# A weight gradient by two-level block products: a new order of visits, and three results stored in halves of columns

## The chip, the core and the metric

The kernel runs on one core of a Trainium2 chip. The metric is device microseconds of that core. Before the change the median of three runs is 162.01 us (161.97 to 162.06).

## The reference

```python
"input": np.random.randn(16, 512, 1024).astype(np.float32)
"grad_output": np.random.randn(16, 512, 768).astype(np.float32)
...
grad_weight = np.einsum('bmk,bmn->kn', input, grad_output)
return grad_weight.astype(np.float32)
```

The batch and the rows fold into one: a product of X transposed (8192 rows by 1024 columns) with G (8192 rows by 768 columns), summed over the 8192 rows. The result is 1024 by 768 in float32, 3.15 MB; the inputs are 58.72 MB.

## The kernel before

**Loads.** The rows come as 32 loads of 256 rows, numbered 0 to 31 (the string `LOADS`). Loads 0 to 3 and 31 are of kind "s": their two groups of 128 rows are multiplied plainly. Loads 4 to 30 are of kind "P": one level of a fast block scheme (seven products in place of eight) is taken over them. GpSimd's queue (POOL) issues the loads with a cast to bfloat16 (lines 170, 171, and 175, 177 for the first ones); each waits for the one eight places before it to land, and later for a free buffer. Only the first 256 rows of X and the first 128 of G come in float32, over the ScalarE and SyncE queues (`xf`, `gf`), and are rounded on the core (line 217).

**Blocks.** The result has four quarters: A, B (first half of the rows), C, D (second half); A and C are the left 384 columns, B and D the right. Each quarter has four blocks of 128 rows, so that C2 is the third block of C. On a "P" load seven products run: A, B, C, and four that feed several quarters, called 1, 5, 6, 7, each again with four blocks. A block product is a matmul of 128 by 128 weights with 384 columns; there are 916, of which those of A1, A2 and a part of B3 are split in two over banks. Products 5, 6, 7, B and C need sums and differences of the load's parts, made by VectorE: `x0`, `x1`, `x2` on X (lines 199, 201, 203) and `g0`, `g1`, `g2` on G (209, 211, 213). They read and write SBUF only. `x2.30` is the third such sum of load 30; B's products of that load need it.

**Banks.** A's four blocks stay in PSUM banks 0 to 2 for nearly the whole run. All others share banks 3 to 7: a visit multiplies a few loads into a bank and then closes it.

**The plan.** The order of everything on TensorE, VectorE, ScalarE and GpSimd (but for the loads) is the string `PLAN`, written out by hand and run from left to right; each engine works off its part of it in order. Its tokens:

- `C2@6.1`: begin a visit of C2 in bank 6, with one product; `C2.2`: two more products in the same bank.
- `vC2` closes a visit on VectorE: it adds the bank to the running sum in SBUF, a 384-column float32 addition of one PSUM and one SBUF block (line 367), or copies (365). `cC2` closes it on ScalarE by a copy (363), where the bank already holds the whole sum.
- `fC2@6` fills bank 6 with C2's sum, by ScalarE (295), so that the visit that follows can be closed by a copy.
- `zcC2.20` sets a fresh bank aside in an extra SBUF block by ScalarE (379); `yC2.20` adds that block to the sum later, on VectorE, both from SBUF (388).
- `x1.4`, `g0.5`: a sum of a load, stage and load number. `r2`: a rounding of the first float32 rows.
- `wC2`: GpSimd adds to C2 what it shares with another product, both in SBUF (395). Without it, VectorE does so while it closes C2 for the last time (360); with it, ScalarE's copy closes the block. When a block of product 5 is closed for the last time, VectorE makes two subtractions (355, 356).

When a block of A, B, C or D is closed for the last time, `store` sends it out (342), all on SyncE's queue, but for the larger part of B3, the last block, which goes over ScalarE's. The first three results leave in two halves of 64 rows each. The last thing of the run is B3, closed in two parts of 256 columns (ScalarE) and 128 columns (VectorE).

Of the kernel before, what the change touches and what calls it, by code (L numbers as in the profile page):

```python
# [9 lines left out]
P = 128  # L10
# [5 lines left out]
    "A0.1 A2.1 C0@7.1 A3.1 C2@6.1 cC0 r0 C3@3.1 C1@4.1 cC2 A1.1 vC3 B1@5.1 cC1 B2@7.1 D3@6.1 r1 D0@3.1 r4 r2 "  # L16
    "D1@4.1 cB1 D1.1 A0.1 B2.1 cD1 D0.1 B0@5.1 cD3 A3.1 vD0 A2.1 r3 A1.1 B3@6.1 vB0 cB2 B3.1 D3@4.1 B0@3.1 "
    "D2@7.1 vD3 D2.2 B0.1 vB3 B1@5.1 cD2 B1.1 A3.1 C3@4.1 vB1 C3.1 C2@6.2 vC3 A2.1 B3@7.1 C1@5.3 B3.1 B0.1 "
    "vC1 A1.2 C2.1 vB3 B1@4.1 D1@5.1 zcC2.20 D1.1 vB1 B2@7.2 A0.1 vB0 A0.1 A2.1 vD1 D3@6.2 D0@4.1 vB2 D0.1 "
    "A3.1 C3@5.1 vD0 D2@3.1 C0@7.2 vD3 C0.2 vD2 C0.1 C3.2 B3@6.2 vC3 B1@3.2 A3.1 vC0 D3@5.2 vB1 A1.2 B2@4.1 "  # L20
    "vD3 B2.1 D2@3.1 A0.1 yC2.20 A0.1 A3.1 D0@7.1 vB2 D0.1 A2.2 vD2 B0@5.2 D1@4.1 vD0 D1.3 vB0 C0@7.2 A3.1 "
    "vD1 A3.1 A1.1 vC0 B3.1 D2@5.3 fC1@7 B3.1 D0@4.1 vD2 D0.1 A0.2 vD0 fD3@5 C1.3 vB3 C1.1 A2.2 g0.4 cC1 "
    "C3@4.1 B2@6.1 fC2@3 B2.1 g1.4 D3.2 fB0@7 vB2 C3.1 C2.1 cD3 C2.1 g2.4 C2.1 x0.4 C2.2 A2.1 12@5.1 cC2 C3.1 "
    "x1.4 A1.2 c12 x2.4 11@6.1 C0@3.1 fC1@5 vC3 B0.3 c11 vC0 A3.1 C1.1 A0.1 B3@6.1 cC1 61@3.1 B1@4.1 vB3 cB0 "
    "B1.2 c61 73@5.1 g0.5 71@6.1 10@7.1 vB1 13@3.1 x0.5 13.1 A1.1 12@4.1 c13 10.1 A3.1 v12 71.1 c10 73.1 "
    "50@3.1 x1.5 c71 50.1 11@4.1 g1.5 51@7.1 c50 51.1 v11 60@6.1 c73 60.1 61@3.1 g0.6 c51 A2.1 53@5.1 v61 "
    "53.1 fC0@4 A0.1 63@7.1 c53 g2.5 63.1 52@3.1 g1.6 52.1 70@5.1 g2.6 70.1 c52 C0.1 x0.6 C0.1 A1.1 A3.1 cC0 "
    "72@3.1 x2.5 72.2 x1.6 70.1 73@4.1 A0.1 c70 x2.6 63.1 60.1 v73 A2.1 c63 B0@5.2 g0.7 c72 B2@4.2 c60 B2.1 "
    "vB0 62@7.1 fC1@3 62.1 g1.7 62.1 B3@6.1 vB2 B3.1 c62 C1.2 g2.7 C2@4.1 fC0@7 vB3 C2.2 f13@5 C1.1 x0.7 A2.1 "
    "A0.1 cC1 C0.1 11@6.1 vC2 11.1 f51@3 A1.1 13.1 v11 13.1 51.2 x1.7 c13 A3.1 53@6.1 cC0 x2.7 53.1 52@4.1 "  # L30
    "c51 52.1 v53 71@5.2 f50@7 C3@3.1 g0.8 C3.1 f12@6 C3.1 50.1 g1.8 50.1 12.1 g2.8 12.2 x0.8 A2.1 C3.1 c12 "
    "A1.1 A3.1 vC3 52.1 71.1 50.1 x1.8 zc52.20 73@6.2 v71 fB1@3 A0.1 61@4.2 x2.8 c50 61.1 72@5.1 v73 72.1 "
    "fB2@7 B1.2 v72 f10@6 B1.2 B2.1 v61 B2.1 cB1 63@5.1 g0.9 63.1 f51@4 10.3 fC2@3 x0.9 10.1 A1.1 cB2 A3.1 "
    "A2.1 g1.9 51.1 zc63.5 x1.9 51.1 62@7.1 c10 g2.9 62.2 x2.9 c51 A0.1 C2.1 v62 fB3@5 C2.1 60@6.2 y63.5 60.1 "
    "fB0@7 B3.2 v60 cC2 B3.1 11@4.2 y52.20 cB3 B0.2 f13@3 g0.10 B0.1 53@6.2 cB0 13.1 x0.10 13.2 f70@7 A3.1 "
    "11.1 g1.10 c13 A1.1 53.1 x1.10 70.1 f52@5 70.1 v11 70.2 A0.1 g2.10 fB2@4 52.1 x2.10 52.1 C1@3.1 c70 v53 "
    "C1.2 c52 B2.1 C3@7.1 vC1 C3.1 f72@5 B2.1 C0@6.1 vC3 C0.1 cB2 C0.1 72.1 g0.11 f73@3 B1@7.2 A2.1 c72 x0.11 "
    "A2.1 A1.1 f71@4 73.2 vC0 73.1 f63@5 71.1 g1.11 71.1 c73 71.1 x1.11 A0.1 72@6.1 c71 g2.11 72.1 63.1 x2.11 "
    "63.1 fB0@4 63.1 v72 61@3.2 c63 61.1 g0.12 B0.1 fC2@6 B0.1 60@5.1 v61 60.1 cB0 A3.1 g1.12 C2.2 v60 12@3.2 "
    "cC2 12.1 x0.12 12.1 fC3@4 B1.1 A1.1 A2.1 f53@5 g2.12 A3.1 vB1 C3.1 f51@6 C3.1 53.1 v12 53.1 cC3 50@7.2 "  # L40
    "x1.12 50.1 fC1@4 50.1 g0.13 A0.1 c53 51.2 x2.12 51.1 C1.1 g1.13 B3@5.1 c51 B3.1 v50 B3.1 f13@3 C1.1 "
    "52@6.1 vB3 52.1 cC1 13.2 x0.13 13.1 f62@4 11@5.2 c13 11.1 x1.13 A0.1 62.1 v52 62.1 f70@3 62.2 g2.13 "
    "61@7.2 c62 x2.13 70.2 v61 fC0@6 70.1 B2@4.2 v11 c70 B2.1 C0.2 vB2 f71@3 C0.1 A3.1 f73@7 10@5.1 g0.14 "
    "10.3 B1@4.1 x0.14 A2.2 zcB1.4 71.2 10.1 x1.14 f51@4 71.1 73.1 g1.14 73.1 c71 x2.14 73.1 51.1 g2.14 51.1 "
    "c73 A1.2 v10 c51 A0.1 B3@7.1 g0.15 cC0 B3.1 A3.1 63@3.1 vB3 fB1@6 63.2 B0@5.1 g1.15 f70@4 B0.1 v63 B0.1 "
    "B1.2 g2.15 72@7.2 cB1 vB0 72.1 70.1 C2@3.1 x0.15 f52@5 C2.3 53@6.2 vC2 53.1 70.1 52.1 v53 52.2 72.1 "
    "x1.15 f11@6 C1@3.2 v72 C1.1 c52 A2.1 A0.1 vC1 c70 13@7.2 60@5.1 yB1.4 f10@3 60.2 g0.16 60.1 11.2 x0.16 "
    "11.1 10.2 c11 13.1 v60 A1.2 f62@4 A3.1 x1.16 A3.1 f71@6 A2.1 v13 50@5.3 g1.16 50.1 f12@7 g0.17 62.2 "
    "zc50.18 62.1 12.1 g1.17 12.1 c62 12.1 g2.16 12.1 x2.16 71.1 fB1@4 71.1 g2.17 C3@5.1 c12 C3.1 x2.15 C3.2 "
    "x0.17 C3.1 10.1 A2.1 C0@7.1 c10 vC3 C0.2 c71 C0.1 x1.17 A3.1 A0.1 fB2@6 x2.17 A0.1 B0@3.1 g0.18 B0.2 "  # L50
    "B2.1 vC0 B2.3 vB0 B1.3 g1.18 C2@7.2 cB1 g2.18 73@5.2 cB2 vC2 73.1 C1@3.1 f61@4 C1.1 x0.18 C1.1 A1.1 "
    "zc73.3 51@6.2 vC1 51.2 C2@5.1 x1.18 fB3@3 61.2 vC2 61.3 x2.18 f53@5 63@7.2 g0.19 63.1 c61 63.1 53.2 v63 "
    "f52@4 53.1 B3.2 g1.19 f12@7 B3.1 v51 B3.1 A0.1 c53 52.1 12.1 cB3 12.1 13@5.1 x0.19 f71@6 13.2 12.1 "
    "72@3.1 x1.19 72.2 v13 72.1 71.2 v12 71.1 70@5.2 g0.20 70.1 f60@7 70.1 52.1 v72 52.2 60.1 g1.20 60.1 c52 "
    "x2.19 60.2 c71 A1.1 v70 A1.1 11@3.1 f10@6 g2.19 11.2 x0.20 11.1 fB3@5 10.3 v11 A3.2 c10 A3.1 x1.20 A2.1 "
    "fB1@3 73@4.1 x2.20 73.2 g0.21 B3.1 60.1 62@6.1 v73 62.1 c60 62.2 g2.20 B1.1 C0@4.1 g1.21 C0.1 cB1 y50.18 "
    "C0.1 C2@7.1 cB3 C2.1 g2.21 B1@3.2 v62 fB2@5 A2.3 x0.21 B2.3 vC0 C2.1 71@6.2 zcC2.1 vB1 A0.1 51@4.1 cB2 "
    "51.1 g0.22 51.1 A0.1 f72@5 50@7.1 v71 50.3 g1.22 50.1 C1@3.2 v50 C1.1 72.2 x1.21 C3@7.2 g2.22 c72 C3.1 "
    "v51 C3.2 C1.1 x0.22 A1.3 zcC1.10 12@6.1 f63@5 12.1 x1.22 12.1 53@4.1 f13@3 53.1 v12 53.2 63.1 x2.21 63.2 "
    "x2.22 63.1 B0@6.1 g0.23 B0.1 c63 B0.2 v53 B0.1 A0.1 vC3 A0.1 f70@4 13.3 f52@5 x0.23 13.1 70.2 c13 70.1 "  # L60
    "g1.23 A3.1 fC0@7 x1.23 A3.1 52.1 vB0 52.3 g2.23 61@3.2 g0.24 61.3 70.1 C0.1 v61 C0.1 c70 C0.1 62@6.1 "
    "y73.3 c52 62.2 cC0 x2.23 B3@4.3 g1.24 f71@5 B3.1 v62 A3.2 A0.1 x0.24 A0.1 A2.3 vB3 71.3 x1.24 73@4.2 "
    "yC1.10 c71 73.2 fB2@7 50@6.1 g2.24 50.1 v73 11@5.3 x2.24 B2.1 f60@4 B2.1 v11 B2.1 f62@3 B2.1 60.1 g0.25 "
    "60.1 cB2 60.2 x0.25 A1.3 72@7.1 x1.25 72.2 g1.25 72.1 A3.1 yC2.1 62.1 zc72.15 62.1 60.1 x2.25 A2.1 "
    "B1@5.1 c60 g2.25 B1.2 c62 B1.2 B0@4.1 f10@3 B0.1 vB1 B0.1 53@7.2 g0.26 53.1 10.2 g1.26 10.2 x0.26 10.2 "
    "51@5.2 c10 x1.26 51.2 y72.15 51.1 f52@3 50.1 A3.1 vB0 zc51.21 50.2 A0.1 x2.26 A0.1 fB2@4 63@5.1 g0.27 "
    "63.3 52.1 g1.27 53.1 v50 B2.2 zc53.18 52.1 v63 52.1 cB2 12@6.2 g2.26 12.2 x0.27 12.1 B3@7.2 g2.27 B3.1 "
    "11@4.1 v12 11.3 y53.18 C0@5.3 vB3 C0.1 C2@6.2 g0.28 fC3@7 C2.3 vC0 C2.1 C3.1 g1.28 C3.2 x1.27 C3.2 vC2 "
    "52.1 61@5.1 cC3 61.1 y51.21 61.1 c52 61.1 A2.1 v11 A2.2 13@6.1 x0.28 13.4 x1.28 72@7.2 zc13.12 72.1 "
    "x2.28 61.1 f73@3 70@4.1 v72 70.2 f71@6 70.1 v61 70.1 73.2 g2.28 73.1 x2.27 73.1 C3@5.1 g0.29 71.4 g1.29 "  # L70
    "A2.1 C1@7.1 c71 g2.29 C1.2 c73 x0.29 C1.4 A3.1 g0.30 A3.1 zcC1.4 A3.1 C3.1 f11@3 v70 A1.4 x1.29 f62@4 "
    "12@7.1 g1.30 12.1 A0.1 y13.12 A0.2 11.1 vC3 11.1 10@6.2 x0.30 10.2 11.1 13@5.1 v10 13.1 c11 12.1 62.1 "
    "x1.30 f61@6 62.2 v12 62.1 f72@3 62.1 61.1 v13 f71@7 61.1 A2.1 v62 72.1 f60@5 72.1 71.1 v61 71.1 f51@4 "
    "60.2 g2.30 60.1 f52@6 60.1 v72 60.1 51.2 v60 f70@3 51.1 wC2 51.1 52.1 v71 52.2 A3.1 f63@7 v51 A3.2 70.1 "
    "fC0@5 70.1 63.2 yC1.4 63.1 wD1 63.1 C0.1 v70 C0.1 fC1@4 C0.2 v63 C0.1 A0.2 vC0 fD1@7 A0.1 C1.2 v52 fC2@5 "
    "C1.1 A2.2 f73@3 A1.3 vC1 fB1@6 wD2 D1.2 x2.30 73.2 cD1 x2.29 B1.2 vA3 B1.1 fB2@7 B1.2 v73 fD2@4 B1.2 "
    "C2.1 vA2 C2.1 f53@3 C2.2 vA1 C2.1 53.2 cC2 53.1 vB1 53.1 B2.1 fC3@5 B2.1 v53 B2.1 fD3@2 B2.3 f50@6 C3.1 "
    "vA0 C3.2 wB3 50.1 vB2 50.3 vC3 D2.1 fB0@7 D2.1 D3.1 v50 D3.1 cD2 B0.2 fD0@5 B0.3 fB3@3+4 vD3 B0.2 D0.2 "
    "vB0 B3.4 vD0 B3.2 cB3 "
# [18 lines left out]
}  # L98


HALVED = 3


@with_exitstack
def kernel(
# [6 lines left out]
    nc = tc.nc  # L112
# [340 lines left out]
```

## Time and profile before

| What | Value |
|---|---|
| median of three runs | 162.01 us |
| the profiled execution's own time | 161.87 us |
| its span | 160.1 us |
| loads L170 + L171, 60 issues | 16.7 and 16.9 us from issue to landing |
| VectorE closings L367 | 117, mean 552 ns |
| ScalarE closings L363 and fills L295 | 105 and 103, mean 478 to 485 ns |
| additions of blocks set aside, L388 | 13, mean 549 and 550 ns |
| GpSimd additions, L395 | 4, mean 1061 ns |
| stores of 192 KB on SP | 12, 2.1 us from issue to landing |
| stores of 96 KB on SP | 6, 2.2 us from issue to landing |

The profile takes one execution apart. Busy time is summed by engine (PE is TensorE's matmuls, PEld its weight loads, DVE VectorE, ACT ScalarE, POOL GpSimd, SP SyncE). A group's row has its line, engine, operation, output and inputs by the program's names, the number of instructions, their total and mean. A bracket `[0.45 <-DVE xp L203]` gives the idle time before an instruction and what ended it. Instructions of one engine overlap a little, so that the time from one start to the next can be shorter than a duration: VectorE's 384-column additions last 0.55 us and start 0.466 us apart when nothing holds them. "DMA share" is the mean busy share of the core's 16 DMA engines. The granted TensorE clock is full over the whole span.

### The profile page before, as it was taken

How to read it: one execution, taken by the hardware profiler on the slowest of the kernel's cores; microseconds unless marked ns; L12 is line 12 of the kernel's file. 1: busy time of each engine (PE TensorE's matmuls, PEld its weight loads, DVE VectorE, ACT ScalarE, POOL GpSimd, SP SyncE). 2: the span in 40 equal slices, each digit the busy share in tenths (PEclk: the TensorE clock that was granted, in tenths of full speed). 3: DMA queues.
4: the chain of work that ended last, by engine and by line, in shares of the span. 5: the costliest groups of instructions: out<-in, count | busy, mean ns of one | idle time of the engine just before them, and what ended most of it. 6: DMA issues, size and time to landing. Idle time of an engine off the chain costs nothing.

```text
span 160.1 us, 2989 instructions
## 1 busy us (share of the span) xinstructions
PE 154.8 (97%) x1002; PEld 98.9 (62%) x1129; DVE 145.1 (91%) x335; ACT 99.3 (62%) x227; POOL 39.1 (24%) x73
## 2 busy tenths in 40 slices
PE   8999999999999999999999999999999999999891
PEld 3466666567677777776656566666666566666461
DVE  0579899999999999999999999999989999999991
ACT  3741028779699998985785756365465244586760
POOL 7442212222221222222122222212222100024120
PEclk9999999999999999999999999999999999999999
DMA  5999999999999999999999999999999999930696
GB/s 176 296 211 212 214 215 215 212 213 216 209 214 214 212 211 214 214 213 214 213 214 213 213 212 212 214 214 209 214 214 212 214 213 214 213 60 18 184 365 218
DMA packets 12446, 33.41 MB, mean 209 GB/s; under 512 B 1424, under 2 KB 4240, under 8 KB 12432
## 3 DMA queue, kind: packets, MB, share of 16 engines
q0 software_dynamic: 9360, 28.64, 90.4%
q1 hardware_dynamic: 2640, 3.41, 6.6%
q10 hardware_dynamic: 432, 1.18, 2.0%
q8 instruction: 8, 0.13, 0.3%
q14 instruction: 6, 0.05, 0.1%
HBM read 58.72 MB, written 3.15 MB: 386 GB/s over the span
## 4 chain that ended last, share of the span: by engine, by line
PE 78%; DMA 16%; POOL 1%; DVE 1%; issue 1%; DVEq 0%; POOLq 0%
PE bank L324 78%; DMA xp<-in_input_dram 16%; POOL gp L175 1%; DVE xp L203 1%; POOL xp L177 0%; DVE acc L365 0%; DVEq L365 0%; POOLq L437 0%
## 5 line engine op out<-in xcount | busy, mean ns | idle before, releaser
L324 PE MATMUL bank<-gp,xp 128*128 128x384 bf16 (+2 forms) x672 | 108.9, 307 | 1.1 <-DVE xp L203 0.5
L324 PEld LDWEIGHTS <-xp 128*128 128x128 bf16 x672 | 61.7, 97 | 32.4 <-DMA xp<-in_input_dram 2.0
L324 PE MATMUL bank<-ge,xe 128*128 128x384 bf16 x324 | 64.0, 326 | 0.0
L324 PEld LDWEIGHTS <-xe 128*128 128x128 bf16 x324 | 31.2, 97 | 15.3 <-DVE xe L201 0.2
L363 ACT COPY macc<-bank 128x384 f32<-128x384 f32 x63 | 28.8, 482 | 17.5 <-PE bank L324 17.3
L367 DVE TENSOR_TENSOR acc<-bank,acc 128x384 f32<-128x384 f32 x62 | 32.4, 552 | 2.8 <-PE bank L324 2.6
L295 ACT COPY bank<-macc 128x384 f32<-128x384 f32 x60 | 28.2, 485 | 6.2 <-DVE macc L367 2.8
L367 DVE TENSOR_TENSOR macc<-bank,macc 128x384 f32<-128x384 f32 x55 | 29.9, 552 | 1.1 <-PE bank L324 0.6
L295 ACT COPY bank<-acc 128x384 f32<-128x384 f32 (+2 forms) x43 | 20.1, 478 | 14.7 <-DVE acc L367 12.1
L171 POOL DMA_DIRECT2D xp<-in_input_dram x30 | 15.9, 532 | 51.9 <-DMA xp<-in_input_dram 22.8
L170 POOL DMA_DIRECT2D gp<-in_grad_output_dram x30 | 16.0, 532 | 38.3 <-PE bank L324 18.8
L363 ACT COPY acc<-bank 128x384 f32<-128x384 f32 (+1 forms) x42 | 19.4, 479 | 8.2 <-PE bank L324 7.8
L199 DVE TENSOR_TENSOR xe<-xp 128x1024 bf16<-128x1024 bf16 x27 | 18.5, 685 | 0.1
L209 DVE TENSOR_TENSOR ge<-gp 128x768 bf16<-128x768 bf16 x27 | 14.8, 550 | 0.3 <-DMA gp<-in_grad_output_dram 0.3
L203 DVE TENSOR_TENSOR xp<-xp,xe 128x512 bf16<-128x512 bf16 x27 | 11.7, 440 | 0.2
L201 DVE TENSOR_TENSOR xe<-xe,xp 128x512 bf16<-128x512 bf16 x27 | 11.3, 419 | 0.3
L379 ACT COPY aside<-bank 128x384 f32<-128x384 f32 x13 | 6.2, 479 | 8.0 <-PE bank L324 7.8
L323 PEld LDWEIGHTS <-xp 128*128 128x128 bf16 x81 | 7.9, 98 | 4.8 <-DMA xp<-in_input_dram 0.4
L395 POOL TENSOR_TENSOR acc<-acc,macc 128x384 f32<-128x384 f32 x4 | 4.2, 1061 | 22.8 <-DVE macc L360 16.5
L211 DVE TENSOR_TENSOR ge<-gp,ge 128x384 bf16<-128x384 bf16 x27 | 9.5, 352 | 0.2
L213 DVE TENSOR_TENSOR gp<-ge,gp 128x384 bf16<-128x384 bf16 x27 | 9.5, 351 | 0.1
L360 DVE TENSOR_TENSOR acc<-bank,macc 128x384 f32<-128x384 f32 (+2 forms) x14 | 6.3, 489 | 0.1
(23 smaller groups left out, 37.6 us busy)
## 6 DMA issues: line engine op xcount, KB each, us to landing
xp<-in_input_dram POOLq DMA_DIRECT2D x30, 512.0 KB, 16.9
gp<-in_grad_output_dram POOLq DMA_DIRECT2D x30, 384.0 KB, 16.7
out_dram<-acc SPq DMA_DIRECT2D x12, 192.0 KB, 2.1
xf<-in_input_dram ACTq DMA_DIRECT2D x2, 512.0 KB, 4.9
gp<-in_grad_output_dram POOLq DMA_DIRECT2D x3, 192.0 KB, 6.5
out_dram<-acc SPq DMA_DIRECT2D x6, 96.0 KB, 2.2
xp<-in_input_dram POOLq DMA_DIRECT2D x2, 256.0 KB, 7.8
gf<-in_grad_output_dram SPq DMA_DIRECT2D x2, 192.0 KB, 4.4
```

The lines of the kernel that those rows point to most:

```text
L170: nc.gpsimd.dma_start(out=gp, in_=G[rows, :].rearrange("(p m) n -> p m n", m=2))
L171: nc.gpsimd.dma_start(out=xp, in_=X[rows, :].rearrange("(p m) k -> p m k", m=2))
L199: nc.vector.tensor_sub(out=xe[:, 0:2, :], in0=x[:, 1::-1, :], in1=x[:, 3::-2, :])
L201: nc.vector.tensor_sub(out=xe[:, 2, :], in0=xe[:, 0, :], in1=x[:, 0, :])
L203: nc.vector.tensor_add(out=x[:, 1, :], in0=x[:, 2, :], in1=xe[:, 2, :])
L209: nc.vector.tensor_add(out=ge[:, 0:2, :], in0=g[:, 0:2, :], in1=g[:, 1::2, :])
L211: nc.vector.tensor_add(out=ge[:, 2, :], in0=g[:, 3, :], in1=ge[:, 0, :])
L213: nc.vector.tensor_add(out=g[:, 1, :], in0=ge[:, 2, :], in1=g[:, 2, :])
L295: nc.scalar.copy(out=tile_[:, t0 : t0 + c1 - c0], in_=sum_of(p, q)[:, c0:c1])
L324: nc.tensor.matmul(tile_[:, t0 : t0 + c1 - c0], stat, mov[:, c0:c1], start=start, stop=True, skip_group_check=True,)
L363: nc.scalar.copy(out=d, in_=b)
L367: nc.vector.tensor_add(out=d, in0=b, in1=d)
```

## The change

The plan is a new one from end to end: the same 916 block products, the same six sums of each of the 27 "P" loads, the same loads in the same order. It has 143 visits instead of 158, 125 closings on VectorE instead of 146, 101 instead of 105 on ScalarE, 99 fills instead of 102, 20 blocks set aside and added instead of 13, and three additions on GpSimd instead of four. The roundings of the first rows, that stood ahead of the plan, are now tokens of it. Around GpSimd's additions: before, `yC1.4` stands between `wC2` and `wD1`, and `x2.30` and `x2.29` a few tokens behind `wD2`; now no `y` follows `wC1`, `x2.30` stands behind `wC1` and two closings, and `g2.30` behind `wC2` and one. Three results leave in halves: the first, the second and the tenth, by 192 columns of all 128 rows instead of 64 rows of all columns. A fill of 128 columns (there is one, for B3) is made by VectorE instead of ScalarE.

The plan's beginning and end, before and after, and the code:

```diff
 PLAN = (
-    "A0.1 A2.1 C0@7.1 A3.1 C2@6.1 cC0 r0 C3@3.1 C1@4.1 cC2 A1.1 vC3 B1@5.1 cC1 B2@7.1 D3@6.1 r1 D0@3.1 r4 r2 "
...
-    "x1.30 f61@6 62.2 v12 62.1 f72@3 62.1 61.1 v13 f71@7 61.1 A2.1 v62 72.1 f60@5 72.1 71.1 v61 71.1 f51@4 "
-    "60.2 g2.30 60.1 f52@6 60.1 v72 60.1 51.2 v60 f70@3 51.1 wC2 51.1 52.1 v71 52.2 A3.1 f63@7 v51 A3.2 70.1 "
-    "fC0@5 70.1 63.2 yC1.4 63.1 wD1 63.1 C0.1 v70 C0.1 fC1@4 C0.2 v63 C0.1 A0.2 vC0 fD1@7 A0.1 C1.2 v52 fC2@5 "
-    "C1.1 A2.2 f73@3 A1.3 vC1 fB1@6 wD2 D1.2 x2.30 73.2 cD1 x2.29 B1.2 vA3 B1.1 fB2@7 B1.2 v73 fD2@4 B1.2 "
-    "C2.1 vA2 C2.1 f53@3 C2.2 vA1 C2.1 53.2 cC2 53.1 vB1 53.1 B2.1 fC3@5 B2.1 v53 B2.1 fD3@2 B2.3 f50@6 C3.1 "
-    "vA0 C3.2 wB3 50.1 vB2 50.3 vC3 D2.1 fB0@7 D2.1 D3.1 v50 D3.1 cD2 B0.2 fD0@5 B0.3 fB3@3+4 vD3 B0.2 D0.2 "
-    "vB0 B3.4 vD0 B3.2 cB3 "
+    "r11 r10 r16 r15 r14 r13 C1@7.1 A3.1 cC1 A2.1 C2@5.1 A1.1 cC2 r0 r12 D3@7.1 B0@6.1 r4 r2 B2@5.1 cD3 B2.1 "
...
+    "f63@7 52.1 x1.28 52.1 73@6.1 g1.29 73.2 v70 73.1 63.2 v73 63.2 A2.1 x0.29 A3.1 c63 C0@3.2 A1.2 f62@7 "
+    "x1.29 10.2 x2.29 10.1 11@6.1 vC0 11.3 x2.26 11.1 f12@3 62.1 v52 62.1 c10 62.2 g0.30 62.1 f61@4 12.2 "
+    "g2.29 f13@5 12.1 yC2.20 12.1 A0.2 g1.30 13.2 x0.30 13.1 11.1 A2.1 c13 61.1 x1.30 A3.1 12.1 f71@5 v11 "
+    "61.2 c12 62.1 71.1 v61 71.1 f60@6 71.2 x2.28 10@3.1 f51@4 60.1 v71 60.3 v10 60.1 f72@5 wC1 60.1 51.1 v62 "
+    "51.2 72.1 v60 f73@7 72.2 x2.30 A1.2 f63@6 A1.1 v72 A2.1 f70@3 A2.1 v51 A3.1 f52@5 wC2 A3.1 63.2 52.2 v63 "
+    "73.1 fC1@4 73.1 70.1 g2.30 70.1 fB1@6 v73 A0.2 C1.1 v70 C1.1 f53@7 C1.2 vA3 B1.2 cC1 B1.1 v52 B1.1 fC3@3 "
+    "B1.3 fC2@4 53.1 C3.1 vB1 C3.1 fD1@5 C3.2 vA2 fB2@6 C3.1 A0.1 53.1 vC3 53.1 C2.2 v53 C2.2 D1.2 cC2 B2.2 "
+    "vD1 B2.1 wB3 f50@4 B2.2 vA1 fC0@7 B2.2 50.1 vA0 fD2@3 50.3 vB2 fD3@0 C0.3 v50 fB0@5 C0.1 D2.2 fD0@6 B0.2 "
+    "vD2 B0.3 vC0 B0.1 fB3@3+4 B0.1 D0.2 vB0 D3.2 B3.1 vD0 B3.4 vD3 B3.2 cB3 "
 ).split()
...
-HALVED = 3
+HALVED = (0, 1, 9)
...
-    round_by("DVE", g0, gf, 0, 192)
-    round_by("ACT", g0, gf, 192, NH)
-    round_by("DVE", x0, xf[0], 0, P)
-    round_by("ACT", x0, xf[0], 2 * P, 4 * P)
-    round_by("DVE", x0, xf[0], P, 2 * P)
-    round_by("DVE", x0, xf[0], 4 * P, 6 * P)
-    round_by("ACT", x0, xf[0], 6 * P, 8 * P)
...
+    ROUNDINGS = {
+        0: ("DVE", g0, gf, NH, N),
...
+        10: ("DVE", g0, gf, 0, 192),
+        11: ("ACT", g0, gf, 192, NH),
+        12: ("DVE", x0, xf[0], 0, P),
+        13: ("ACT", x0, xf[0], 2 * P, 4 * P),
+        14: ("DVE", x0, xf[0], P, 2 * P),
+        15: ("DVE", x0, xf[0], 4 * P, 6 * P),
+        16: ("ACT", x0, xf[0], 6 * P, 8 * P),
+    }
...
-            nc.scalar.copy(out=tile_[:, t0 : t0 + c1 - c0], in_=sum_of(p, q)[:, c0:c1])
+            copy = nc.vector.tensor_copy if c1 - c0 == 128 else nc.scalar.copy
+            copy(out=tile_[:, t0 : t0 + c1 - c0], in_=sum_of(p, q)[:, c0:c1])
...
-        halves = [slice(0, P)]
-        if len(stored) < 2 * HALVED:
-            halves = [slice(0, P // 2), slice(P // 2, P)]
-        for rows in halves:
-            stored.append(rows)
-            queue.dma_start(out=OUT[rows, row, at : at + c1 - c0], in_=sum_of(p, q)[rows, c0:c1])
+        cuts = [c0, (c0 + c1) // 2, c1] if stored[0] in HALVED else [c0, c1]
+        stored[0] += 1
+        for a, b in zip(cuts, cuts[1:]):
+            queue.dma_start(out=OUT[:, row, at + a - c0 : at + b - c0], in_=sum_of(p, q)[:, a:b])
```

The weight loads of some blocks are issued twice in a middle part of the run (line 323); this is as before.

## The prediction

> **What bounds the kernel now.** I read the busy shares first, then the chain that ended last, then the instructions around its one piece that is not TensorE, then the waits, then the end in windows.
>
> ```profile
> PE 154.8 (97%) x1002; PEld 98.9 (62%) x1129; DVE 145.1 (91%) x335; ACT 99.3 (62%) x227; POOL 39.1 (24%) x73
> DMA  5999999999999999999999999999999999930696
> ```
>
> TensorE is busy nearly throughout, the DMA engines from 4 to 140 us, VectorE 91%: three resources close to full. The chain in order of time:
>
> ```profile
> 12.20 17.80 DMA xp<-in_input_dram
> 30.00 0.05 issue
> 30.05 117.88 PE bank L324 x776
> 147.93 1.24 DVE xp L203 x2
> 149.17 0.05 issue
> 149.22 7.51 PE bank L324 x51
> ```
>
> Up to 30 us TensorE follows the loads. From 30.05 it runs on its own, but for 1.24 us spent on two VectorE sums. The timeline there (start, length, engine):
>
> ```profile
> 147.54 1.00 POOL L395 TENSOR_TENSOR acc<-acc,macc 128x384 f32<-128x384 f32 x1 [1.54 <-DVE macc L356]
> 147.84 1.31 DVE L203 TENSOR_TENSOR xp<-xp,xe 128x512 bf16<-128x512 bf16 x2
> 149.22 1.15 PE L324 MATMUL bank<-gp,xp 128*128 128x384 bf16 x6 [0.45 <-DVE xp L203]
> ```
>
> A GpSimd addition runs while VectorE makes two sums of SBUF blocks. All 27 runs of that sum, from the view of its line:
>
> ```profile
> L203 DVE TENSOR_TENSOR xp<-xp,xe x27: 412/418/979, 26.9 to 148.7; 128x512 bf16<-128x512 bf16 x27
> ```
>
> Minimum, median, maximum: 979 ns is the one beside GpSimd, 0.56 over the median. TensorE waited: matmul starts stand 778 ns apart instead of 162.5, a loss of 0.62 us. Waits of weight loads on input:
>
> ```profile
> PEld L324 <- DMA xp<-in_input_dram: 2.0, 6, 0.7
> PEld L324 <- DVE xp L203: 1.3, 3, 0.8
> ```
>
> The end (length; clock, DMA share, GB/s):
>
> ```profile
> 150.00:152.00 2.00, 1.00 0.74 206
> 152.00:157.00 5.00, 1.00 0.99 361
> 157.00:160.10 3.10, 1.00 0.55 184
> ```
>
> The stores keep the DMA engines full for the last five microseconds of matmuls.
>
> **The floor that the loads set.** Both plans hold 916 block products of 384 columns, 162.5 ns each start to start (162 or 163 in the trace). No plan can end before a load's landing plus the products that it has left from that load's first use (counted in the plan, 0.05 us from landing to matmul). Landings are the trace's:
>
> - load 5, 30.00: 770 products left before, 771 after: 155.18 and 155.34
> - load 8, 42.94: 692 and 691: 155.44 and 155.28
> - load 29, 134.11: 132 and 131: 155.61 and 155.45
> - load 30, 138.42: 106 and 104: 155.70 and 155.37
>
> Load 7 (38.63) gives 155.35 in both. The floor is 155.70 before and 155.45 after: -0.25. The last matmul of before ends at 156.72, which is 1.02 above its floor: 0.62 is the stall shown, 0.40 is spread in steps of 0.03 to 0.06 us over a hundred microseconds.
>
> **The change, part by part.**
>
> *Start.* The right half of the first gradient lands at 6.35, is rounded in 0.36, and frees TensorE at 6.78 in either order. Before, eight products stand ahead of that point, now five: 0.49 us behind. Three products later B2 needs the second gradient rows, which land at 7.51; TensorE would be there at 7.27: 0.28 more, 0.77 in all. The first cast ahead of a matmul is 256 columns (0.29) instead of 128 (0.23): 0.05, inside the wait for 6.78. Five waits for input of 0.17 to 0.66 follow before 30.1 (the weight loads' idle times), and they hide all of it: from 7.56 the 23.2 us before load 5's first use end at about 29.95, before 30.05. Cost 0; with that cover gone, up to 0.77. This is so thin a cover (0.1 us) that I keep +0.2 for the range.
>
> *VectorE.* Closings by VectorE fall from 146 to 125, additions of blocks set aside rise from 13 to 20, and one 128-column fill moves to it. Start to start a closing or such an addition takes 0.466 in the trace, so 14 fewer are -6.5 us: 137.0 to 130.5. That is queue length, not path. ScalarE has 105+102+13 closings, fills and set-asides before and 101+99+20 after: 220 both times. Its work is 62% of the span, and I cost it at nothing; VectorE's shorter queue covers the fills' inputs. The load queue of GpSimd keeps its order.
>
> *The stall.* Before, the sums of loads 30 and 29 stand in VectorE's queue a few products ahead of B1's products with these loads. Now load 29's sum stands 19.7 us of products before the end, load 30's 12.5, and the first product that needs the latter comes 25 products (4.1 us) later. GpSimd's three additions wait for VectorE's closings of 71, 72 and 53. I add VectorE's queue at 0.466 per closing (0.93 for a 5-block, 0.53 for A1 and A2, 0.335 and 0.265 for the late sums), in us before the last matmul's end: 71 ends at 14.05, so the first addition (1.00) runs to 13.05, and the sum of load 30 starts at 12.73; 72 ends at 11.85, the second runs to 10.85, and the last g sum starts at 10.53. Margins 0.32 both. The third meets only closings, which read PSUM and one SBUF block. The 0.62 goes. What is late next: the loads, 0.40 above their floor. For the new order's own small waits I take the same 0.40, the nearest row; the ends are 0 and before's whole 1.02. So the last matmul ends at 155.45 + 0.40 = 155.85: **-0.87**.
>
> The Trainium skill, page "SBUF — State Buffer", section "Who interferes with whom", says that VectorE with two SBUF inputs and a reading GpSimd instruction exclude each other, and that the second to issue waits for the first to finish. By that rule the sum issued at 147.84 would have waited 0.70 and ended at 148.95; the trace has 148.82, so its 0.57 decides, and the removed stall stays 0.62.
>
> *The end.* Before, GpSimd merged four blocks (C2, D1, D2, B3), which ScalarE then only copied; now three (C1, C2, B3), and one closing more is VectorE's, counted above. The last three additions (B0, D0, D3) start about 1.6, 1.13 and 0.67 before the last matmul's end, so D3 is in SBUF at about -0.1 and its store is issued then; D0's in before was issued at 156.54, -0.18. The last copy and its SP store follow the last matmul as now (157.17). SP has 19 issues before and after, 0.49 apart when queued (151.55, 152.04, 152.53). The halves by rows landed 0.62 to 0.70 apart for 96 KB, the whole results 0.53 to 0.55 for 192 KB. Halves by columns use 128 partitions in 768-byte packets. The trace has 27 ns for 512, 48 for 1024 and 65 for 1536 bytes, so about 38 for 768: 0.60 per result, +0.06 each, where before's cost +0.7. But the first store now starts 8.7 before the last matmul's end instead of 10.2, and the stream is full at 0.99. These nearly cancel; I take **+0.13** (0.08 for the later D3, 0.05 for queueing). Ends: -0.2 when the earlier gain counts alone; +0.75 when a 768-byte packet costs the full 65 ns.
>
> **Sum.** The profiled execution took 161.87 around its span of 160.1. 161.87 - 0.87 + 0.13 = 161.13. It lies 0.14 under the median of the runs shown (162.01), so in their terms 161.27: **161.3**.
>
> **The rivals.**
>
> *Contention returns.* A margin of 0.32 is less than one closing. If a late sum meets an addition again, VectorE loses 0.57 and TensorE, with closings queued behind it, up to 0.62: 161.9. For it: the margins; against: the sum of load 30 is needed 4.1 us later, so only bank releases behind it suffer. By the same page's section the whole rest of the addition, up to 1.0, would be lost; 162.3 by that, not used. Chance 0.10.
>
> *The stores end it.* With 65 ns for a 768-byte packet, three results cost 0.54 more each, 1.6 in all on a full stream; some 0.9 of it falls into gaps while results are awaited, and 0.75 stays instead of 0.13: 161.9. For it: the share of 0.99; against: the 512-byte row. Chance 0.12.
>
> *VectorE becomes the bound: slower.* Place: the ninth stretch of 10 us of products (10.16 us of time), where the new order puts 10.3 us on VectorE (closings at 0.466, the sums of a load at 0.60, 0.33, 0.34, 0.47, 0.27 and 0.27 start to start); before's worst is 10.1. If closings there took their row's 0.552, ten of them add 0.9; the stretches from 120 to 140 (9.9 and 9.7) would add another 1.0 over their time. Less the 0.40 already counted, +1.5: 162.8. It decides from 1.46 us above the floor on. For it: 91% busy; against: before has 9.0 to 10.1 in thirteen such stretches and lost 0.40 in all. Chance 0.15.
>
> **How the numbers follow.** A measurement of this kernel tells about 0.2% (0.32 us) from no change: 161.69 to 162.33. My forecast has 0.63, with its own range 160.8 (nothing above the floor) to 161.7. Contention and stores, 0.22, fall within "same"; VectorE's 0.15 is slower. The range 160.8 to 162.3 leaves out that 0.15 and a little below.
>
> **What would show it.** Right: no wait of TensorE on the late sums; every GpSimd addition near 1.00 and no L203 sum near 0.98; first matmuls stalling until 6.8 and 7.55; the load-5 wait near 30.0 shrunk to 0.1 or so; last matmul near 155.9. Wrong: steps of TensorE on ScalarE's fills after 80 us, a last matmul after 156.5, a last store over 2.6 us behind the last matmul.

## The result, and the profile after

The changed kernel takes 163.16 us in the median of 22 runs (161.77 to 163.52), the kernel before 161.94 us in 22 runs beside them (161.88 to 162.18): 1.0054 of it, 95% interval 1.0034 to 1.0073. It is slower, by half a per cent and clear of the noise; the forecast was 161.3 us. The time of the changed kernel lies at two levels, 15 runs at 163.04 to 163.52 and 7 at 161.77 to 162.00, with the granted clock full in both. The profiled execution took 163.04 us around a span of 161.3, so it is one of the higher level.

From the page of the changed kernel: busy times, one DMA queue (packets, MB, share of 16 engines over the span), GpSimd's additions.

```profile
PE 155.3 (96%) x1003; PEld 99.5 (62%) x1130; DVE 139.1 (86%) x322; ACT 99.0 (61%) x226; POOL 37.8 (23%) x72
...
q8 instruction: 8, 0.13, 0.3%
...
L393 POOL TENSOR_TENSOR acc<-acc,macc 128x384 f32<-128x384 f32 x3 | 3.0, 1000 | 23.9 <-DVE macc L358 18.7
```

The view of the line of the late sums (minimum, median, maximum in ns; the edits moved line 203 to 202):

```profile
L202 DVE TENSOR_TENSOR xp<-xp,xe x27: 414/418/426, 28.2 to 144.6; 128x512 bf16<-128x512 bf16 x27
```

What the change is about happened: VectorE is busy 6.0 us less, GpSimd's three additions take 1.00 us each, and none of these sums is longer than 0.43 us (before 0.98). Yet the last matmul ends at 157.74 us, before at 156.72. The waits of TensorE on X (in all, times, longest):

```profile
PEld L324 <- DMA xp<-in_input_dram: 2.1, 4, 1.5
...
PE bank L324 <- DMA xp<-in_input_dram: 1.1, 1, 1.1
```

Four weight loads wait, not six, but one for 1.5 us. It is here, in the timeline of TensorE from 19.2 to 22.6 us, first of the changed kernel, then of the kernel before:

```profile
19.01 1.79 PE L324 MATMUL bank<-gp,xp 128*128 128x384 bf16 x10
21.94 0.99 PE L324 MATMUL bank<-gp,xp 128*128 128x384 bf16 x5 [1.14 <-DMA xp<-in_input_dram]
```

```profile
19.01 3.91 PE L324 MATMUL bank<-gp,xp 128*128 128x384 bf16 x26
```

Start to start TensorE loses 1.30 us there. It waits for the X part of load 3, which GpSimd issued at 7.8 us in both kernels. Each load reports its landing in 16 shares, as many as there are DMA engines, and the trace has the time of each. Before, the 16 of this load land by 20.54; after, 15 land by 20.53 and the last at 21.89. The DMA queues from 19 to 21 us say what is new, after and then before:

```profile
q0 software_dynamic: 130, 0.39, 100.0%
q8 instruction: 1, 0.02, 2.9%
```

```profile
q0 software_dynamic: 136, 0.41, 103.1%
```

One packet of kind "instruction", 16,384 bytes, runs from 19.85 for 0.94 us; one share of load 3 comes late behind it. The kernel before has it too, from 21.36, when load 3 is in; there it strikes the gradient part of load 4 (15 shares by 22.36, the last at 23.48), which nobody needs yet. There are eight such packets in either run. In the changed kernel the second to the eighth start 213 to 262 recorded TensorE instructions apart, 247 on average: I take them for refills of TensorE's instruction stream, and a run below bears that out. The Trainium skill, page "Runtime: NRT & Kernel Launch", section "Instruction fetch mechanics", says that a sequencer fetches blocks of 256 instructions, 16 KiB, over a DMA queue of its own, at a cost that is "mostly hidden". The size here agrees, and the spacing nearly; the first one is not hidden.

The end, in windows (length, busy time of PE, PEld, DVE, ACT, POOL, clock, DMA share, GB/s):

```profile
150.00:152.00 2.00, 2.00 (x15) 1.21 (x13) 2.00 (x6) 1.22 (x3) 0.19 (x1) 1.00 0.66 215
152.00:157.00 5.00, 4.93 (x33) 3.03 (x32) 5.00 (x13) 3.04 (x8) 0.82 (x1) 1.00 0.95 338
157.00:161.30 4.30, 0.74 (x10) 0.53 (x8) 0.85 (x3) 0.37 (x1) 0.00 (x0) 0.82 0.65 222
```

The first store is issued at 148.90, 8.8 us ahead of the last matmul's end; from that end to the end of the span it is 3.53 us, before 3.39; the granted clock falls only at 159.73, after the last matmul. And TensorE has new short losses: 0.12 and 0.22 us at 42.7 to 43.4, and 0.24 at 154.5. Around the first two (start, length):

```profile
42.44 0.48 ACT L361 COPY macc<-bank 128x384 f32<-128x384 f32 x1 [0.97 <-PE bank L324]
42.82 0.49 ACT L295 COPY bank<-macc 128x384 f32<-128x384 f32 x1
...
43.36 0.48 PE L324 MATMUL bank<-ge,xe 128*128 128x384 bf16 x2
```

By the plan, the matmul at 42.97 begins a visit in the bank that this closing on ScalarE empties, and the one at 43.36 uses the bank that the fill behind the closing writes. Around the third:

```profile
153.57 0.55 DVE L358 TENSOR_TENSOR acc<-bank,macc 128x384 f32<-128x384 f32 x1
153.69 1.31 ACT L295 COPY bank<-acc 128x384 f32<-128x384 f32 x3 [0.30 <-DVE acc L358]
```

The matmul that starts at 154.64 uses the bank that the second of these three fills writes; the first of them waited 0.30 us for VectorE's closing.

### The profile page after: what moved, and what is told of

It is laid out like the page before. It is cut to its first block, busy times and chain, and to the rows that moved or that the text cites. A ratio compares the mean times of both kernels' runs of the same rounds, so it can differ in the third digit from the quotient of the medians.

```text
span 161.3 us, 2971 instructions
## 1 busy us (share of the span) xinstructions
PE 155.3 (96%) x1003; PEld 99.5 (62%) x1130; DVE 139.1 (86%) x322; ACT 99.0 (61%) x226; POOL 37.8 (23%) x72
## 5 line engine op out<-in xcount | busy, mean ns | idle before, releaser
L324 PE MATMUL bank<-gp,xp 128*128 128x384 bf16 (+2 forms) x673 | 110.7, 307 | 1.6 <-DMA xp<-in_input_dram 1.1
L324 PE MATMUL bank<-ge,xe 128*128 128x384 bf16 x324 | 65.7, 326 | 0.1
L361 ACT COPY macc<-bank 128x384 f32<-128x384 f32 x67 | 30.9, 483 | 15.3 <-PE bank L324 14.8
L324 PEld LDWEIGHTS <-xe 128*128 128x128 bf16 x324 | 31.0, 97 | 14.3 <-DVE xe L200 0.3
L295 ACT COPY bank<-macc 128x384 f32<-128x384 f32 x65 | 30.8, 487 | 8.5 <-DVE macc L365 3.8
L365 DVE TENSOR_TENSOR acc<-bank,acc 128x384 f32<-128x384 f32 x46 | 24.6, 552 | 7.2 <-PE bank L324 6.8
L365 DVE TENSOR_TENSOR macc<-bank,macc 128x384 f32<-128x384 f32 x49 | 26.7, 553 | 2.4 <-PE bank L324 1.7
L361 ACT COPY acc<-bank 128x384 f32<-128x384 f32 (+1 forms) x34 | 15.9, 477 | 19.6 <-PE bank L324 19.0
L295 ACT COPY bank<-acc 128x384 f32<-128x384 f32 (+1 forms) x34 | 16.1, 481 | 5.6 <-DVE acc L365 3.7
L377 ACT COPY aside<-bank 128x384 f32<-128x384 f32 x20 | 9.5, 482 | 6.8 <-PE bank L324 6.8
L323 PEld LDWEIGHTS <-xe 128*128 128x128 bf16 x50 | 4.9, 98 | 3.3 <-issue 0.3
```

The costliest lines, as they stand in the source:

```text
L295: copy(out=tile_[:, t0 : t0 + c1 - c0], in_=sum_of(p, q)[:, c0:c1])
L323: nc.tensor.ldweights(stat)
L324: nc.tensor.matmul(tile_[:, t0 : t0 + c1 - c0], stat, mov[:, c0:c1], start=start, stop=True, skip_group_check=True,)
L361: nc.scalar.copy(out=d, in_=b)
L365: nc.vector.tensor_add(out=d, in0=b, in1=d)
L377: copy(out=aside[i], in_=b[:, t0 : t0 + NH])
```

## The experiments

All ratios are to runs of the kernel before on the same chip. "Refill" is the start of the first packet of 16,384 bytes on queue q8 and "last share" the landing of the sixteenth share of load 3's X, both in us from the span's start. "Loss" is the step from one matmul start to the next at TensorE's wait for load 3, less the usual 0.1625 us. Refills, shares and losses are of the one profiled execution of each kernel.

### The two levels, and the refill

**The changed kernel again**, unaltered.

> The changed kernel once more, unaltered. Its runs fall at two levels, 161.8 to 162.0 and 163.0 to 163.5. Theory F (fetch): in the profiled run a 16,384-byte packet of TensorE's instructions (queue 8) started at 19.85 us on one DMA engine, while X of load 3 was in flight; 15 of its 16 shares had landed by 20.53, the last at 21.89, and TensorE, ready for it at 20.5, lost 1.3 us. In a run of the lower level that packet must start after X of load 3 has landed (as in the kernel before: 21.36 against 20.54) and TensorE must not wait 1.3 us there. Rival C (clock): the level is set by when the granted clock becomes full (4.97 us before, 6.13 in the profiled run after); then a run of the lower level shows a full clock from 5 us on and no change of the packet. Expected time by F: the same two levels, about one run in three low.

163.25 us, 1.0056 [1.0028, 1.0083]; two of eight runs at 161.79 and 161.84, six at 163.05 to 163.44. Refill 20.13, last share 22.17, loss at 20.6: 1.42 us. The two levels belong to the kernel, and the trace of the higher one repeats. Rival C does not fit: in the four profiles of the unaltered changed kernel (two more follow below) the granted clock becomes full at 3.73, 6.13, 6.30 and 6.50 us, the first of them sooner than in the kernel before (4.97), and all four are of the higher level.

**Need load 3 later.** Six products of load 2 stand ahead of load 3's first product; for that, two blocks exchange banks 3 and 7.

```diff
-vC1 D3.2 vB1 D3.2 A3.1 B3@3.1 cD3 B3.1 D1@4.2 ... D0@7.2 ... D2@6.1 fC3@5 D2.1 g0.4 D2.2 B0@3.2
+vC1 D3.2 vB1 D2@6.2 D0@3.2 D1@4.2 D3.2 A3.1 cD3 B3@7.1 ... fC3@5 g0.4 D2.2 B0@7.2
```

> The changed kernel, with six products of load 2 (of D0, D1, D2) moved ahead of the first product of load 3, banks 3 and 7 exchanged until D0 closes. Theory F: the packet of instructions still delays X of load 3 to about 21.9 in some runs, but TensorE needs it 0.98 us later (21.5), so the high level falls by 0.9 to 1.2 us onto the low one: all runs 161.7 to 162.3. Rival C (clock at the start) or any cause that is not load 3's landing: two levels as before, 161.9 and 163.2.

163.30 us, 1.0084 [1.0071, 1.0097], all four runs above 163.1: the forecast of my own theory missed. Refill 20.07, last share 22.08; the wait there fell to 0.14 and 0.20 us, but TensorE lost 0.62 at 22.5 and 0.53 at 26.7:

```profile
23.77 1.49 DVE L365 TENSOR_TENSOR acc<-bank,acc 128x384 f32<-128x384 f32 x3 [2.40 <-PE bank L324]
...
26.97 0.35 DVE L212 TENSOR_TENSOR gp<-ge,gp 128x384 bf16<-128x384 bf16 x1
...
27.37 0.65 PE L324 MATMUL bank<-gp,xp 128*128 128x384 bf16 x3 [0.37 <-DVE gp L212]
```

VectorE stands idle for 2.40 us, since the visits that it closes now end late, and its sums of load 4 follow late. To fill TensorE's wait with other products moved the wait to VectorE's queue. This run does not tell the theories apart.

**20 more TensorE instructions** in the changed kernel: weight loads issued twice, ahead of the products 21, 23, ... 59.

```diff
-SPARE_LOADS = range(200, 455)
+SPARE_LOADS = [*range(20, 60), *range(200, 455)]
```

> The changed kernel with 20 weight loads issued twice among the first 60 matmuls, so that TensorE reaches the 256th instruction some 20 instructions (about 1.5 us) earlier. Theory F: the packet starts at 17 to 19 us, always before X of load 3 has landed, the engine that carries it stays about 1 us late, and every run is at the high level or above (163.0 to 163.8). Rival C: the same two levels.

163.07 us, 1.0069 [1.0057, 1.0081], all five runs at 162.90 to 163.17. The later refills come 1.2 to 1.6 us sooner (39.60 for 40.91, 55.82 for 57.07, 71.03 for 72.61), so they do follow TensorE's instructions; the first hardly moved (19.80), where theory F expected 17 to 19 us. Last share 21.88, loss 1.20. There is no lower level among these five runs.

**40 more TensorE instructions in the kernel before**, whose plan is untouched.

```diff
-SPARE_LOADS = range(200, 455)
+SPARE_LOADS = [*range(20, 100), *range(200, 455)]
```

> The kernel before, with 40 weight loads issued a second time between its 20th and 100th product; the arithmetic is the same. Theory F (what cost the change its time is the first refill of TensorE's instructions, a packet of 16,384 bytes that takes one DMA engine for 0.94 us; it hurts when it starts before the X part of load 3 has landed, at 20.54): 40 more instructions ahead of that point bring the first refill from 21.36 to 20.4 or earlier, the last share of load 3's X lands near 21.9 instead of 20.54, TensorE waits 1.0 to 1.4 us there, and the time is 162.7 to 163.3. Rival P (the wait belongs to the new plan's products around load 3): the old plan is untouched and the extra weight loads lie beside matmuls, 161.8 to 162.1. If the first refill does not move ahead of 20.5, nothing is decided.

162.41 us, 1.0026 [1.0017, 1.0035]: slower, by 0.48 in the medians. Refill 19.05, last share 21.38, and where the kernel before ran through there is a wait:

```profile
20.09 0.81 PE L324 MATMUL bank<-gp,xp 128*128 128x384 bf16 x4
...
21.42 0.82 PE L324 MATMUL bank<-gp,xp 128*128 128x384 bf16 x4 [0.52 <-DMA xp<-in_input_dram]
```

The loss is 0.68 us, less than forecast: the last share lands 0.78 us behind the fifteenth, where it is 1.26 to 1.60 behind with refills at 19.80 to 20.28 in the changed kernel. That an earlier refill leaves its engine time to catch up would explain this and is not shown. The wait for load 5 (0.42 at 29.6) is gone, so that the last matmul is 0.45 later. The extra weight loads themselves bring TensorE to load 3 only 0.10 later. An early refill alone makes the old plan slow: rival P falls.

That wait for load 5 in the unaltered kernel before is of the same kind: fifteen shares of its X are in by 29.55, the last at 30.00, and TensorE is ready at 29.63. The prediction's row "load 5, 30.00" thus rests on a late share too.

**40 more in the changed kernel**, the same edit.

> The changed kernel with the same 40 weight loads issued a second time between its 20th and 100th product as were put into the kernel before, where they brought the first refill to 19.05, the last share of load 3's X to 21.38 and a wait of 0.68 us. Theory F (both levels are this refill: it strikes load 3's last packets, or comes behind them): the refill comes at 18.2 to 19.2 in every run, always ahead of load 3's end and never right at it, the share lands at 21.3 to 21.5, the wait is 0.6 to 0.9 us instead of 1.3 to 1.5, and there is one level, 162.4 to 162.8. Rival L (the two levels come from something else than the refill): two levels as before, 161.8 to 162.0 and 163.0 to 163.5.

162.69 us, 1.0043 [1.0029, 1.0057], all five runs at 162.50 to 162.89: one level, between the two. Refill 18.53, last share 21.48, loss 0.67:

```profile
19.23 1.79 PE L324 MATMUL bank<-gp,xp 128*128 128x384 bf16 x10
21.52 1.69 PE L324 MATMUL bank<-gp,xp 128*128 128x384 bf16 x10 [0.51 <-DMA xp<-in_input_dram]
```

More work made the changed kernel faster in the median and took the two levels away, with the refill moved. That is what theory F says and rival L does not.

### What sets the start of the refill

**Fewer instructions ahead of load 3** in the changed kernel.

```diff
-C3@4.2 A2.2 zcC3.4 A1.2 B3.1 ... D1.2 A1.1 B2.1 ... fC2@6 C3.1 A2.1 g2.4
+C3@4.2 zcC3.4 B3.1 ... D1.2 A1.3 B2.1 ... fC2@6 C3.1 A2.3 g2.4
```

> The changed kernel, whose last products of A1 and A2 with load 2 (two each, 16 instructions of TensorE, 0.65 us) stand behind load 3's first products instead of ahead of them. TensorE comes to its wait for load 3 at about 19.9 with 16 instructions fewer behind it. Theory F1 (the refill comes after a count of instructions, so the one that struck load 3 cannot be asked for while TensorE stands at that wait): the refill starts after 20.5, load 3's X lands whole at 20.55, TensorE waits some 0.6 us instead of 1.3, all runs lie at 161.7 to 162.2. Theory F2 (the refill's start is set by something else, near 19.9 whatever TensorE has done): last share at 21.9, wait of 1.9 us, 163.0 to 163.7. A third way is two levels as in the unaltered changed kernel.

163.76, 163.97, 163.99 and 162.56 us; 1.0096 [1.0058, 1.0135]. Refill 19.93, last share 21.94, loss 1.68. Two levels remain, each some 0.6 us higher, about the 0.65 us of work that now stands behind the wait. A count of instructions executed does not set the start of this refill here (about 196 at its start, 208 in the unaltered kernel, 226 with 20 more, 222 with 40 more, 231 before).

**Two more profiles** of the unaltered changed kernel.

> The changed kernel unaltered, for one more profile: the two so far were of the higher level. If this one is of the lower (161.8 to 162.0, 7 of 22 runs and 2 of 8): the refill starts after 20.5, load 3 lands at 20.55, the 1.3 us wait at 20.5 is gone or under 0.3, and the last matmul ends 1.1 to 1.3 us sooner, at 156.4 to 156.6, still 0.6 later than the 155.85 forecast. If of the higher: as before, 163.0 to 163.5.

> The changed kernel unaltered, for a further profile; as for the one ahead of it: lower level with the refill after 20.5 and the last matmul at 156.4 to 156.6, or higher level with both as before.

163.51 and 163.32 us, both of the higher level: refills 20.28 and 20.12, last shares 22.32 and 22.17, losses 1.54 and 1.30. All four profiled runs of the changed kernel were of that level, as 23 of its 32 runs are, so the lower one stands in no trace. What its runs do show is the span: 160.0 to 160.2 us in all nine. Less the 3.53 us between the last matmul and the end, that puts the last matmul at 156.5 to 156.7 (an estimate); the four traces of the higher level, each less its loss at load 3, have it at 156.4 to 156.7.

**One wait of the sequencer**, out of the changed kernel and into the kernel before.

```diff
-r11 r10 r16 r15 r14 r13 C1@7.1 A3.1 cC1
+r11 r10 r16 r15 r14 r13 C1@3.1 A3.1 cC1
```

> The changed kernel whose very first visit (C1, one product) takes bank 3 instead of bank 7, the bank that the warm-up wrote; nothing else. That removes one instruction of TensorE, a separate wait of its sequencer for the end of the warm-up, that the kernel before does not have. Theory W (that stop of the sequencer shifts the refills, so that the first comes near 19.9 to 20.3 and strikes load 3): the first refill starts after 20.7, load 3's X lands whole at 20.55 to 20.8, the wait near 20.6 is under 0.3 us, all runs lie at 161.7 to 162.1. Rival R (the start of the refill comes from the order of products or the loads): two levels as before, 161.8 to 162.0 and 163.0 to 163.5, most runs at the higher one.

```diff
-A0.1 A2.1 C0@7.1 A3.1
+C0@7.1 A0.1 A2.1 A3.1
```

> The kernel before with its third product (C0, bank 7) put first, ahead of A0 and A2; nothing else. That adds the same separate wait of TensorE's sequencer for the end of the warm-up. Theory W: the first refill moves from 21.2 to 21.4 to before 20.5, load 3's last share lands at 21.4 to 22.2, TensorE waits 0.7 to 1.4 us there, and runs (all or most) lie at 162.4 to 163.2. Rival R: refill at 21.2 to 21.4 as before, 161.8 to 162.1.

Changed kernel: 162.00 once and 163.17 to 163.58 five times, 1.0073 [1.0047, 1.0098]; refill 20.23, last share 22.24, as ever. Kernel before: 162.01 us, 1.0004 [0.9995, 1.0013]; its refill did move, to 20.32, but load 3 was whole at 20.45 and nothing was lost: the late share was one of load 4's G (fifteen by 22.29, the last at 23.34). So a refill shortly ahead of load 3's landing need not strike it, though one at 20.28 in the changed kernel did. Theory W falls. Why the first refill comes near 20.0 in the one kernel and near 21.3 in the other stays open.

### The end

**The two late sums moved forward** in the kernel before, some 50 products, out of the way of GpSimd's additions.

```diff
-... v12 62.1 f72@3 ... 72.1 f60@5 72.1 ... D1.2 x2.30 73.2 cD1 x2.29 B1.2
+... v12 62.1 x2.29 f72@3 ... 72.1 f60@5 x2.30 72.1 ... D1.2 73.2 cD1 B1.2
```

> The kernel before, with the last two sums of X (loads 29 and 30) moved ahead by some 50 products, away from GpSimd's additions; nothing else. Prediction's price for the contention: 0.62 us of TensorE's waiting goes and nothing takes its place, 161.95 - 0.6 = 161.35. Rival: TensorE's waits on fills and banks behind VectorE's queue take most of it, 161.8 to 162.0.

162.42 us, 1.0029 [1.0018, 1.0040]: slower, against both forecasts. The stall at 148.4 is gone, but the sums now stand ahead of closings:

```profile
141.20 0.95 ACT L295 COPY bank<-macc 128x384 f32<-128x384 f32 x2 [0.30 <-DVE macc L367]
141.55 0.41 DVE L203 TENSOR_TENSOR xp<-xp,xe 128x512 bf16<-128x512 bf16 x1
141.73 0.48 PE L324 MATMUL bank<-ge,xe 128*128 128x384 bf16 x2 [0.28 <-ACT bank L295]
```

TensorE loses 0.44 and 0.17 us there, and the last matmul comes only 0.16 sooner (156.56). The first store goes out at 147.11 instead of 146.56; from there on one store follows another, whole results 0.51 to 0.55 us apart in landing, and the last lands at 159.61 instead of 159.18: 12.5 us after the first store's issue, before 12.6.

**No GpSimd addition for D2** in the kernel before; **column halves alone** in it; **both**.

```diff
-vC1 fB1@6 wD2 D1.2 x2.30 ... D3.1 cD2 B0.2
+vC1 fB1@6 D1.2 x2.30 ... D3.1 vD2 B0.2
```

```diff
-        halves = [slice(0, P)]
-        if len(stored) < 2 * HALVED:
-            halves = [slice(0, P // 2), slice(P // 2, P)]
-        for rows in halves:
-            stored.append(rows)
-            queue.dma_start(out=OUT[rows, row, at : at + c1 - c0], in_=sum_of(p, q)[rows, c0:c1])
+        cuts = [c0, c1]
+        if len(stored) < HALVED:
+            cuts = [c0, (c0 + c1) // 2, c1]
+        stored.append(p)
+        for a, b in zip(cuts, cuts[1:]):
+            queue.dma_start(out=OUT[:, row, at + a - c0 : at + b - c0], in_=sum_of(p, q)[:, a:b])
```

> The kernel before without GpSimd's addition for D2, the one that runs beside the two late sums; VectorE does it while it closes D2 (one closing more for it, one copy fewer for ScalarE). The slow sum of 0.98 us and TensorE's 0.62 us wait go, the last matmul ends at 156.1 to 156.3. Theory S: the first store stays at 146.6, so the last landing stays near 159.1: 161.8 to 161.9. Rival T: the whole gain shows, 161.3 to 161.5.

> The kernel before, whose first three results leave in halves of columns instead of rows; nothing else. Theory S (the stream of stores, not TensorE, sets the end: from the first store's issue to the last landing it took 12.6 us before and 12.5 with the two sums moved forward, whatever TensorE did): row halves landed 0.62 to 0.70 us apart, column halves 0.48 to 0.50, so six of them give some 0.9 us back, of which only what lies above TensorE's own tail shows: 161.5 to 161.8. Rival T (TensorE's last matmul sets the end, stores follow it): 161.9, no change, last matmul at 156.7 in both.

> Both at once: no addition for D2 on GpSimd, and the first three results in halves of columns. Theory S: the parts together give more than their sum, since the stream of stores ends some 0.9 us sooner and TensorE's tail 0.5 us sooner: 161.2 to 161.4. Rival T: as without the column halves, 161.3 to 161.5, and equal to that run within 0.1.

| Kernel | us | ratio [95%] | last matmul ends | from there to the end of the span |
|---|---|---|---|---|
| before | 161.93 | | 156.72 | 3.39 |
| no addition for D2 | 161.78 | 0.9987 [0.9978, 0.9996] | 156.35 | 3.79 |
| column halves | 162.00 | 1.0000 [0.9991, 1.0008] | 156.56 | 3.36 |
| both | 161.62 | 0.9978 [0.9969, 0.9987] | 156.22 | 3.64 |

The line of the sums without the addition for D2:

```profile
L203 DVE TENSOR_TENSOR xp<-xp,xe x27: 415/421/426, 27.2 to 148.4; 128x512 bf16<-128x512 bf16 x27
```

No slow sum, and TensorE's 0.62 falls to 0.05; the last matmul comes 0.36 sooner (in this execution, the slowest of its eleven, load 5 lands at 30.26 instead of 30.00, which takes 0.26 of the gain), and the stores take all of it back: they go out with a single pause over 0.25 us until 156.93 (before 157.17, with two such pauses in the last 2.5 us) and the last lands at 159.22 (before 159.18). So theory S holds where TensorE comes sooner, and rival T where only the stores get shorter: with column halves alone (96 KB landing 0.47 to 0.50 apart instead of 0.62 to 0.65) the stores run into pauses in which no result is ready. Each hides behind the other, and both together are the fastest kernel here, by 0.31 us in the medians and not by the 0.5 to 0.7 forecast: at its end the chain stands on VectorE's last closings. From that chain (start, length):

```profile
43.22 111.64 PE bank L324 x734
154.85 1.39 DVE acc L360 x3
```

**Row halves again** in the changed kernel.

```diff
-        cuts = [c0, (c0 + c1) // 2, c1] if stored[0] in HALVED else [c0, c1]
+        halves = [slice(0, P // 2), slice(P // 2, P)] if stored[0] in HALVED else [slice(0, P)]
         stored[0] += 1
-        for a, b in zip(cuts, cuts[1:]):
-            queue.dma_start(out=OUT[:, row, at + a - c0 : at + b - c0], in_=sum_of(p, q)[:, a:b])
+        for rows in halves:
+            queue.dma_start(out=OUT[rows, row, at : at + c1 - c0], in_=sum_of(p, q)[rows, c0:c1])
```

> The changed kernel with its three halved results cut by rows again (64 rows of all columns); nothing else. Two levels as in the changed kernel, so the end is read from the trace: from the last matmul to the end of the span it took 3.56 us with column halves. If the stream of stores sets the end (first store at 148.9, last landing 11.3 us later), three results of row halves take some 0.2 us per half more, of which up to 1.2 shows: 4.0 to 4.7. If the column halves are worth nothing, as in the kernel before, where they changed this from 3.39 to 3.34: 3.5 to 3.6.

164.03 and 164.04, and 162.44, 162.63 and 162.82 us: both levels some 0.7 higher (1.0058 [1.0021, 1.0094]). From the last matmul to the end of the span 4.28 us instead of 3.53. The stores of 96 KB (median us to landing), with row halves, then with column halves:

```profile
out_dram<-acc SPq DMA_DIRECT2D x6, 96.0 KB, 2.2
```

```profile
out_dram<-acc SPq DMA_DIRECT2D x6, 96.0 KB, 1.7
```

In this order, whose first store starts 1.3 us closer to the last matmul, the halves lie on the path, and their cut is worth 0.75 us.

## Why the prediction was wrong

- **The floor that the loads set** is the step that failed. "Landings are the trace's" took them as fixed, and load 3 stood in no row, since its 20.54 gave only 154.65 (20.54 + 0.05 + 825 products of 162.5 ns). In the changed kernel it lands at 21.89, and 828 products are left: 156.49, above every row that I listed and 1.04 above the 155.45 that I used. The refill that does it is in the profile of before too, one of 8 packets on a queue with 0.3% of the DMA engines' time, 0.82 us behind load 3's landing (21.36 and 20.54): I passed that row over. That a refill ahead of load 3's landing costs this time is shown by moving it in the kernel before. That the lower level is the runs in which it misses load 3 is argued, from the one level that the 40 weight loads leave and from the size: 1.3 us between the levels, 1.30 us lost. What decides from run to run, and what sets the first refill's start, stays open.
- **The 0.40 above the floor** was too little: the profiled run ends 1.25 above its floor of 156.49. 0.58 of that are the closing and the fills of ScalarE at 43 and 154 us. That ScalarE costs nothing and "VectorE's shorter queue covers the fills' inputs" is wrong by these 0.58; "steps of TensorE on ScalarE's fills after 80 us" stood among the signs of a wrong forecast, and the one at 154.5 is such a step. They are about what the lower level (161.8 to 162.0) lies above 161.3. The reading of before's 0.40 was loose as well: from load 30's landing on, 0.15 lies ahead of its first product (138.62), 0.09 in short steps beside the stall, and 0.16 in the end of the last matmul; the hundred microseconds ahead of it do not enter.
- **The start** came out as said: ahead of load 3 the changed kernel is some three products behind (88 done by 20.48 us, before 91), and less the 1.30 lost at load 3, TensorE would come to load 5's first product at 29.95 (31.25 in the profile), as forecast. In the other three profiles of the changed kernel the same sum gives 30.12 to 30.23, up to 0.18 past the 30.05 of before; the 0.2 kept for the start would have been needed there.
- **VectorE**: 6.0 us less busy, against 6.5 of queue; it became no bound in the middle.
- **The stall** went and no addition met a sum: right, the margin of 0.32 was 0.22 in the trace (the addition ends at 144.42, the sum of load 30 starts at 144.64) and was enough. But its 0.62 is not worth 0.62. Taken out of the kernel before alone it gave 0.21 us (0.06 to 0.36, by the ratio), and in its profile the stores end no sooner; the sum carried TensorE's gain to the end one to one.
- **The end**: +0.14 against +0.13, with the first store 8.8 us before the last matmul (8.7 forecast). The two halves of that step were also right: row halves would have cost 0.75 more here, and column halves do nothing where results come late. Their 768-byte packets took 36 ns, where I had estimated 38.
- **The rivals**: contention did not return, the stores did not end it. The third, VectorE as the bound, named the right sign for another reason, which is luck. None of the three was a load that lands late; with the loads named as the floor, a late landing belonged among them.

## What to carry to other kernels

A floor made of landings is only as firm as the landings: for every load list the time between its landing and its first use, and ask what else uses a DMA engine in that time, instruction packets of TensorE included. A refill can make one share of a load late by its own length and more, and the matmul waits for the slowest share. Where TensorE's tail and a full stream of stores end together, take time from both or expect to see little of it.

## What was not expected of the hardware

- A 16,384-byte instruction packet of 0.94 us made the share of the load it struck land 1.36 us behind the other fifteen; in before, load 4's by 1.12. One share stayed late over the following loads: in the changed kernel by 1.07 for load 4's X (24.80 and 25.87) and by 1.02 for load 5's (29.16 and 30.18), in before by 0.88 for load 4's X (24.81 and 25.69).
- Refills from the second on came 247 recorded TensorE instructions apart on average (213 to 262). The first began at 208 executed instructions in the changed kernel and at 231 in the kernel before. In the changed kernel its time stayed at 19.80 to 20.28 us when 12 fewer or 18 more had run, and went to 18.53 us, at 222, with 40 weight loads more.
- Two levels 1.3 us apart at a full granted clock: 9 of 32 runs of the changed kernel, of which four were profiled and none of those was low.
